# Second layer's experts: high and low parts as 128 stationary columns, and the product down spread over the next expert's steps

## The chip, the cores and the metric

The kernel runs on one core of one Trainium2 chip. The metric is the device time of one execution, in microseconds. Three runs of the kernel before took 2166.81, 2170.14 and 2172.33 us; the median, 2170.14 us, is the time that the change is held against. TensorE is PE (its weight loads PEld), VectorE is DVE, ScalarE is ACT, GpSimd is POOL and SyncE, which issues the loads of weights, is SP.

## The reference

Two layers, each with four mixers (Hyena, S5, RWKV, Mamba), a gated merge of their outputs and a mixture of 16 experts, on 256 latent and 256 context tokens of 1024 channels. The second layer has no context output. The change lies in the experts:

```
def moe_ffn(u, w_group, w_expert, w_gate, w_up, w_down):
    ...                          # groups by softmax, two experts of a group for each token
    comb = jnp.sum(jax.nn.one_hot(e_idx, MOE_EXPERTS, dtype=F32) * top_w[..., None], axis=-2)
    y = jnp.zeros_like(u)
    for e in range(MOE_EXPERTS):
        h = jax.nn.silu(u @ w_gate[e]) * (u @ w_up[e])
        y = y + comb[..., e:e + 1] * (h @ w_down[e])
    return y
```

For each expert w_gate and w_up are 1024 x 512 and w_down is 512 x 1024, all float32. In the second layer an expert's list has 64 places, so at most 64 tokens are computed in the main pass.

## The kernel before

A large float32 product is made of three products of shorter operands: each operand is split into a high part (a cast that rounds, on ACT, L299) and a low part (the operand less its high part, on DVE, L300), and `mm3` (L320) adds high by high, high by low and low by high in a bank of PSUM.

An expert has twelve chunks of weights of 512 KB each: four of gate, four of up, four of down (L1371 `expert`). Each chunk is loaded by SP into one of 21 buffers `raw`, taken in turn, cast by ACT into `wh` and subtracted by DVE into `wl`. There are three pairs of `wh` and `wl`, taken in turn, so ACT can cast a chunk only when PE has finished with the chunk three before it. PE then multiplies.

For gate and up the tokens are stationary and the weights move: the token columns `xx` of the expert (64 columns of the high or of the low part) are loaded as weights of the array, and 512 columns of `wh` or `wl` stream past them. A chunk holds two blocks of 128 channels, so it takes six matmuls of 512 columns. The result has 64 rows (tokens) and 512 columns. ACT takes the tanh of half the gate (L1403), DVE makes gate and up into h by two operations (L1404, L1405), PE transposes h in four pieces (L334) and ACT and DVE split the transposed 128 x 256 into `hh` and `hl`. For down `hh` and `hl` are stationary; a chunk takes six matmuls of 512 columns into two banks. ACT and DVE scale the two halves of the result into `yo` (L1417, L1418), and POOL scatters the rows to `Y` in memory (L1419).

The loop over experts (L1627 to L1646) sets the order: of each expert, three steps of gate (one chunk each), then the whole product down of the expert before it, then one further step of gate and four of up. With the fourth step `entries` (L1558) makes the list of the expert after next: which tokens, where they go (`ri`) and their weights (`rf`), each in a pool of four buffers. `ri` is read by the scatter of its expert. In the second layer `gather` (L1595) makes the token columns `xx` of four experts at a time by products with a matrix of picks; it runs beside experts 2 to 5, 6 to 9 and 10 to 13, in steps, and the last experts run without it.

The first layer's experts go through the same loop, with lists of 112 places and `xh`, `xl` in place of `xx`. A scheduler orders the instructions of each engine from the whole program by its own estimates; on the chip each engine takes them in that order and waits for what an instruction needs.

Of the kernel before, what the change touches and what calls it, by code (L numbers as in the profile page):

```python
# [24 lines left out]
# tiles of 128 columns of w_in: Hyena, S5, RWKV (r, k, v, wd | ad), Mamba (z, x, B, C), gates, then gd | dt  # L25
T_HY, T_S5, T_RW, T_WA, T_M2, T_GT, T_GDT, NTILE = 0, 6, 8, 14, 15, 23, 55, 56
EPS = 1e-6
AHEAD = 3
AH2 = 5
# [47 lines left out]
NQS = (2, 4)  # pairs of groups in a part of S5  # L77
# [3 lines left out]
# ---------------------------------------------------------------- constants of the shapes  # L81


def _cst():
# [16 lines left out]
    # N^T of two-token blocks, rows s, columns t; backward scans in partitions 0..63  # L101
# [15 lines left out]
    # places less 1024  # L117
# [3 lines left out]
    # a token's row in U, and in Y2 for its first and second expert; Y2's less that of the rows without a token  # L121
    c["tok"] = np.stack([tok + 1.0, tok, tok + 512.0, tok - 1024.0], 2).reshape(128, 16)
    # resets of the running sums at the ends of 64-token chunks
# [7 lines left out]
def _rows():  # L131
    """rows of the modulation in groups of 32 (context, latent; the bias in the first's third): to each token's stream, to latent"""
    half = np.r_[np.ones(64), np.zeros(64)]
    m = np.zeros((128, 2, 128))
    for p in range(0, 128, 32):
        m[p:p + 2, 0] = half, 1 - half
        m[p + 1, 1] = 1
    m[2] = 1
    return m.reshape(128, 256)
# [39 lines left out]
def pack(inp):  # L179
    """Lays the inputs out for the loads; no arithmetic on them."""  # L180
# [32 lines left out]
    # S5: rows (second index of a pair of groups, state), columns (part, direction, pair)  # L213
# [44 lines left out]
class K:  # L258
# [27 lines left out]
    def banks(self, **n):  # L286
        """the banks of PSUM by tag"""
# [9 lines left out]
    # ---- float32 operands of the large products in two parts of 12 bits: a b = ah bh + al bh + ah bl  # L297
# [4 lines left out]
    def raw(self, ap):  # L302
        """1024 columns of weights"""
# [7 lines left out]
    def wsplit(self, ap, k):  # L311
        """the parts of 1024 columns of weights (k by 1024 / k)"""
# [18 lines left out]
    def tr(self, out, in_, base=0):  # L331
        """out = in_^T on the tensor engine"""
# [6 lines left out]
    def rsqrt(self, pool, out, x, tag):  # L339
        """out = x ** -0.5 by Newton's iteration from the exponent's half; x > 0, small tiles"""  # L340
# [11 lines left out]
    def proj(self, l, t, xm, c0, c1, n=128):  # L352
        """p^T of w_in's tile t: n columns in partitions, tokens c0..c1"""
# [6 lines left out]
    # ------------------------------------------------------------------ RWKV-7  # L360
    def rwkv(self, l, xm, pc, dtT, yT, ctx_out, beside):
        """yT[:, hp, :]: the mixer's output, channels in partitions; columns 0..255 context, 256.. latent.
        dtT: Mamba's dt, from the tile that has both's columns, with tokens in partitions"""
        v, s, g, c = self.v, self.s, self.g, self.c
        with ExitStack() as es:
# [23 lines left out]
            def shifted(ps, n, j, out):  # L389
                """p + (mean of its neighbours - p) mu"""  # L390
# [20 lines left out]
            lo = {0: 64, 1: 0}  # partitions of the solves  # L411
# [4 lines left out]
            own = {d: slice(lo[d], lo[d] + 64) for d in range(2)}  # columns of a direction in the pairs' matrices  # L416
# [8 lines left out]
            for hp in range(2):  # L425
# [3 lines left out]
                # kappa: k k_k over its norm in the head  # L429
# [7 lines left out]
                # block diagonal pairs, of directions or heads: -b~ and k~ against kappa~, and the solves' (later M)  # L437
# [5 lines left out]
                for st in range(2):  # L443
# [6 lines left out]
                    for d in range(2):  # L450
                        dh = 2 * d + hp
                        # decay in log, its running sum in each chunk, and W = exp of that
# [21 lines left out]
                        s.activation(cum, cum, AF.Exp, scale=-1.0)  # 1 / W  # L474
# [16 lines left out]
                        # products of a chunk's tokens, masked: rows k~ and b~ (b~ and k~ backward)  # L491
# [11 lines left out]
                    # (I - N)^-1 of every chunk, N = -tril(kappa~ beta~^T): pairs of blocks, doubling  # L503
# [8 lines left out]
                    def each(a, b, us=range(8)):  # L512
                        """a^T b of the pairs"""
# [18 lines left out]
                    # tokens in partitions: v above (below) the solves, kappa~, and [k~; -b~]  # L532
# [33 lines left out]
                    # per chunk: H' = W_T (M H + k~^T v - b~^T u0), and y's reading of H  # L566
# [15 lines left out]
                    # the states that chunks enter (block diagonal), the last one that of the next stream's first chunk  # L582
# [23 lines left out]
                    # y^T  # L606
# [10 lines left out]
                    # group norm over a head, bonus, gate  # L617
# [24 lines left out]
    def headscale(self, pool, sq, f, eps, is_max, ni):  # L642
        """(f * sum over a head of sq, with eps added or as its least) ** -0.5, over the head's partitions"""
# [29 lines left out]
    def silu(self, x, t):  # L673
        """x = silu(x), with a scratch like it"""
# [4 lines left out]
    # ------------------------------------------------------------------ Mamba-2  # L679
    def mamba(self, es, l, xm, pc, yT, ctx_out, dtT):  # L680
# [4 lines left out]
        if True:  # L685
# [10 lines left out]
            # softplus = max(x, 0) + log1p(exp(-|x|)); log1p(e) = 2 atanh(e / (2 + e))  # L696
# [724 lines left out]
    def moe(self, l, m, x, pool, nt, rows, tabl, U, Y2, e_f, fp, tmp, ready, after):  # L1421
# [99 lines left out]
        with ExitStack() as es:  # L1521
# [33 lines left out]
            with ExitStack() as e2:  # L1555
# [72 lines left out]
                for e in range(16):  # L1628
# [6 lines left out]
                    for j in range(8):  # L1635
                        if j == AHEAD:
                            for _ in prev:
                                pass
# [324 lines left out]
```

## Time and profile before

| | |
|---|---|
| runs of the kernel before | 2166.81, 2170.14, 2172.33 us |
| span of the profiled execution, first to last instruction | 2165.3 us |
| lowest of the three runs less that span | 1.5 us |
| mean granted clock of TensorE, as a share of full | 0.946 |
| PE, DVE, ACT, POOL busy, share of the span | 91%, 76%, 46%, 18% |
| first scatter of the second layer's experts | at 1856.33 us |
| last one | at 2136.72 us |

The profiled execution has no time of its own beside its span; what lies around the span is read off the lowest run. Busy shares are means over all stages. In the second layer's experts the starts of the sixteen scatters mark the experts, one each. A matmul's duration includes its way through the array, so what a row of matmuls costs is the distance between their starts. The granted clock is given per window: 1.00 is 2.4 GHz, 0.50 is 1.2 GHz.

### The profile page before, as it was taken

What the parts mean: (1) busy time and instruction counts of PE and PEld (TensorE: products, weight loads), DVE (VectorE), ACT (ScalarE), POOL (GpSimd) and SP (SyncE); (2) the same over time, 40 slices, a digit from 0 to 9 for tenths busy, and PEclk for the clock granted to TensorE, in tenths of its full rate; (3) what the DMA queues carried; (4) which work ended last, traced back from release to release, by engine and by line L of the source; (5) the groups of instructions that cost most, each with busy time, mean ns of one, the idle gap of its engine ahead of it and who ended that gap; (6) DMA issues with size and microseconds to landing.
All of it is one profiled execution on the core that took longest, in us unless ns stands there. A gap on an engine that the chain in (4) does not pass through costs nothing. (4 is left out here: it accounts for less than half of the span.)

```text
span 2165.3 us, 31795 instructions
## 1 busy us (share of the span) xinstructions
PE 1970.2 (91%) x11290; PEld 1504.7 (69%) x11290; DVE 1651.0 (76%) x3451; ACT 985.5 (46%) x1571; POOL 399.0 (18%) x502
## 2 busy tenths in 40 slices
PE   6999999889999899999995899899798878999994
PEld 2779889567666678777774689897575767555652
DVE  5575675478888777999996686776879776888895
ACT  3321322244344234777773332323434335777783
POOL 1000100033532322102213010100524221010100
PEclk9999999889999898999998899999898988999997
DMA  7221221533444845999993221312434394899981
GB/s 299 78 74 59 74 67 52 197 123 113 156 146 154 313 172 186 362 368 372 372 341 138 84 90 63 98 52 76 160 134 161 129 350 174 304 329 366 330 325 64
DMA packets 131915, 406.28 MB, mean 188 GB/s; under 512 B 18139, under 2 KB 30205, under 8 KB 131361
## 3 DMA queue, kind: packets, MB, share of 16 engines
q1 hardware_dynamic: 125778, 388.34, 50.6%
q0 software_dynamic: 5968, 15.80, 2.3%
q8 instruction: 92, 1.51, 0.3%
q14 instruction: 77, 0.63, 0.1%
HBM read 374.72 MB, written 34.61 MB: 189 GB/s over the span
## 5 line engine op out<-in xcount | busy, mean ns | idle before, releaser
L299 ACT CAST wh<-raw 128x1024 fp32r<-128x1024 f32 x528 | 553.0, 1048 | 537.9 <-PE bank L337 482.9
L300 DVE TENSOR_TENSOR wl<-raw,wh 128x1024 fp32r<-128x1024 f32 x528 | 642.6, 1231 | 146.4 <-ACT wh L299 143.1
L337 PE MATMUL bank<-xmh,wh 128*128 128x512 f32 (+2 forms) x896 | 338.3, 378 | 15.8 <-ACT wh L299 14.7
L337 PE MATMUL bank<-xmh,wl 128*128 128x512 f32 (+2 forms) x896 | 331.0, 370 | 15.4 <-DVE wl L300 15.4
L337 PE MATMUL bank<-xml,wh 128*128 128x512 f32 (+2 forms) x896 | 326.4, 365 | 0.0
L337 PEld LDWEIGHTS bank<-xmh,wh 128*128 128x128 f32 (+1 forms) x896 | 176.7, 197 | 54.2 <-ACT wh L299 19.2
L337 PEld LDWEIGHTS bank<-xmh,wl 128*128 128x128 f32 (+1 forms) x896 | 175.9, 196 | 51.6 <-DVE wl L300 22.2
L337 PEld LDWEIGHTS bank<-xml,wh 128*128 128x128 f32 (+1 forms) x896 | 176.5, 197 | 29.2 <-issue 6.2
L337 PE MATMUL bank<-wh,xx 128*64 128x512 f32 x512 | 168.1, 397 | 0.2 <-ACT wh L299 0.2
L1419 POOL DMA_INDIRECT Y<-yo,ri x32 | 43.4, 1357 | 420.4 <-DVE yo L1418 304.8
L337 PE MATMUL bank<-DD,TB 128*128 128x64 f32 (+1 forms) x848 | 111.5, 273 | 1.3 <-DVE TB L523 0.9
L337 PEld LDWEIGHTS bank<-DD,TB 128*128 128x128 f32 x848 | 106.3, 192 | 6.0 <-DVE DD L598 0.9
L337 PE MATMUL bank<-wl,xx 128*64 128x512 f32 x256 | 102.8, 402 | 1.3 <-DVE wl L300 1.1
L337 PE MATMUL bank<-wl,hh 128*112 128x512 f32 (+1 forms) x256 | 99.9, 396 | 0.0
L337 PEld LDWEIGHTS bank<-wh,xx 128*64 128x64 f32 x512 | 69.6, 136 | 43.1 <-issue 1.4
L337 PE MATMUL bank<-wl,xh 128*112 128x512 f32 x240 | 97.9, 408 | 0.2
L337 PE MATMUL bank<-wh,hl 128*112 128x512 f32 (+1 forms) x256 | 97.4, 400 | 0.5 <-DVE hl L300 0.2
L337 PE MATMUL bank<-wh,xl 128*112 128x512 f32 x240 | 94.8, 395 | 0.9 <-DVE xl L300 0.9
L337 PE MATMUL bank<-wh,xh 128*112 128x512 f32 x240 | 92.8, 395 | 0.8 <-ACT xh L299 0.8
L337 PE MATMUL bank<-wh,hh 128*112 128x512 f32 (+1 forms) x256 | 89.8, 397 | 1.1 <-ACT hh L299 1.1
L337 PE MATMUL bank<-raw,c 128*32 128x256 f32 x768 | 71.3, 423 | 18.6 <-DMA raw<-in_modw_dram 18.6
L337 PE MATMUL bank<-DD,AB 128*128 128x64 f32 x640 | 84.5, 275 | 0.7 <-DVE DD L510 0.7
(547 smaller groups left out, 3799.5 us busy)
## 6 DMA issues: line engine op xcount, KB each, us to landing
raw<-in_mg_dram SPq DMA_DIRECT2D x128, 512.0 KB
raw<-in_mup_dram SPq DMA_DIRECT2D x128, 512.0 KB
raw<-in_mdn_dram SPq DMA_DIRECT2D x128, 512.0 KB
raw<-in_win_dram SPq DMA_DIRECT2D x112, 512.0 KB
raw<-in_modw_dram SPq DMA_DIRECT2D x96, 512.0 KB
GT<-t SPq DMA_DIRECT2D x32, 256.0 KB
raw<-in_wbr_dram SPq DMA_DIRECT2D x16, 512.0 KB
G<-GT SPq DMA_DIRECT2D x8, 1024.0 KB
```

The source lines that it names most:

```text
L299: self.s.copy(hi, src)
L300: (eng or self.v).tensor_tensor(lo, src, hi, OP.subtract)
L337: self.t.matmul(out, lhsT=lhsT, rhs=rhs, start=start, stop=stop)
L1419: g.indirect_dma_start(out=Y2, out_offset=bass.IndirectOffsetOnAxis(ap=to, axis=0), in_=yo, in_offset=None, bounds_check=1023, oob_is_err= ...
```

## The change

Five things change, and all comments and docstrings are gone, which moves line numbers by 2 to 32 lines (L299 is L301 now, L300 is L302, L337 is L339, L1403 to L1405 have L1425 to L1427 beside them).

1. `STEPS` gives the order of steps for each layer, g for a step of the present expert and p for one chunk of the product down of the one before. The first layer's string is the old order. In the second layer the four chunks of down stand apart: after the fourth, fifth, seventh and eighth step.
2. In the second layer `xx` holds an expert's high and low columns side by side, and `both` loads all 128 as stationary, so one matmul with `wh` makes high by high in rows 0 to 63 and low by high in rows 64 to 127. A second matmul of 64 columns adds high by low: two in place of three.
3. The two halves of the rows must be added, and h is needed transposed. ACT copies the 128 x 512 bank of gate and that of up into `gu` (L1420), and eight matmuls of 128 x 64 with two stacked identities (`i64`) add and transpose at once. The four transposes of h are gone; tanh and the two operations of DVE work on 128 x 256 in place of 64 x 512.
4. `ri` and `rf` have eight buffers in place of four.
5. `hh` and `hl` are taken from their pools ahead of the banks of gate and up.

```
+STEPS = ("gggppppggggg", "ggggpgpggpgp")
...
+        stacked = OC[l] and xs is not None
...
+        hh, hl = (tmp.tile([128, 4, cap], F32R, tag="h" + x, bufs=xb[2], name="h" + x) for x in "hl")
+        pg, pu = self.bank(), self.bank()
...
-                    self.mm3(ps, [z[:, kk] for z in xs], (wh[:, k], wl[:, k]), kk == 0, kk == KT - 1)
+                    if stacked:
+                        both = lambda: self.mm(ps, xs[:, kk], wh[:, k], kk == 0, kk == KT - 1)
+                        if kk < KT - 1:
+                            both()
+                        self.mm(ps[0:cap], xs[:, kk, 0:cap], wl[:, k], False, False)
+                        if kk == KT - 1:
+                            both()
+                    else:
+                        self.mm3(ps[0:cap], [z[:, kk] for z in xs], (wh[:, k], wl[:, k]), kk == 0, kk == KT - 1)
                 yield
...
+        if stacked:
+            pt = self.bank()
+            for j, ps in enumerate((pg, pu)):
+                r = tmp.tile([128, 512], F32, tag=f"gu{j}", bufs=1, name="gu")
+                s.copy(r, ps)
+                for k in range(4):
+                    self.mm(pt[:, 256 * j + 64 * k:256 * j + 64 * k + 64], r[:, 128 * k:128 * k + 128], self.c["i64"])
+            pg, pu = pt[:, 0:256], pt[:, 256:512]
+            h = tmp.tile([128, 256], F32, tag="h", bufs=xb[1], name="h")
+            s.activation(h, pg, AF.Tanh, scale=0.5)
+            v.scalar_tensor_tensor(h, h, 1.0, pg, OP.add, OP.mult)
+            v.scalar_tensor_tensor(h, h, 0.5, pu, OP.mult, OP.mult)
+            self.split(h.rearrange("p (k t) -> p k t", k=4), hh, hl)
...
                 self.mm3(py[b], (hh[:, kc], hl[:, kc]), [x[:, 0, 512 * b:512 * b + 512] for x in (wh, wl)], kc == 0, kc == 3)
+            if kc < 3:
+                yield
...
-                    ri = tmp.tile([128, 2], I32, tag="ri", bufs=4, name="ri")[0:cap]
-                    rf = tmp.tile([128, 1], F32, tag="rf", bufs=4, name="rf")[0:cap]
+                    ri = tmp.tile([128, 2], I32, tag="ri", bufs=8, name="ri")[0:cap]
+                    rf = tmp.tile([128, 1], F32, tag="rf", bufs=8, name="rf")[0:cap]
...
-                    for j in range(8):
-                        if j == AHEAD:
-                            for _ in prev:
-                                pass
-                            if e < 14:
-                                rec.append(turn("g", entries, e + 2, picks[e + 2]) if OC[l] else entries(e + 2))
+                    j = 0
+                    for z in STEPS[l]:
+                        if z == "p":
+                            next(prev, None)
+                            continue
+                        if j == AHEAD and e < 14:
+                            rec.append(turn("g", entries, e + 2, picks[e + 2]) if OC[l] else entries(e + 2))
```

On PE, in one of the last experts, the kernel before has the four transposes of the expert before, the end of the third step of gate, and then the product down in one block (xx: gate and up; hh and hl: down; 64x512 is the shape of the result):

```order
L334 MATMUL bank<-cst,h 128x64 x4
L337 MATMUL bank<-wl,xx 64x512
L337 MATMUL bank<-wh,xx 64x512 x2
L337 MATMUL bank<-wl,xx 64x512
L337 MATMUL bank<-wh,xx 64x512
L337 MATMUL bank<-wh,hh 64x512 x2
L337 MATMUL bank<-wl,hh 64x512 x2
L337 MATMUL bank<-wh,hl 64x512 x2
L337 MATMUL bank<-wh,hh 64x512
L337 MATMUL bank<-wl,hh 64x512
L337 MATMUL bank<-wh,hl 64x512
L337 MATMUL bank<-wh,hh 64x512
```

In the changed kernel the fourth step of gate ends and the first chunk of down follows; the first four matmuls of it are `hh` alone:

```order
L339 MATMUL bank<-wl,xx 64x512 x2
L339 MATMUL bank<-wh,xx 128x512
L339 MATMUL bank<-wh,hh 64x512
L339 MATMUL bank<-wl,hh 64x512
L339 MATMUL bank<-wh,hh 64x512
L339 MATMUL bank<-wl,hh 64x512
L339 MATMUL bank<-wh,xx 128x512
L339 MATMUL bank<-cst,gu 128x64 x4
L339 MATMUL bank<-wl,xx 64x512
L339 MATMUL bank<-wh,xx 128x512
L339 MATMUL bank<-wl,xx 64x512
L339 MATMUL bank<-wh,hl 64x512 x2
```

The product down no longer stands in one block: two chunks of up come between its matmuls, the products with `hl` come after the first of them, and the four that sum and transpose the `gu` of the gate stand inside that chunk.

On ACT, in the same place, one expert of the kernel before is, from the two casts ahead of the tanh on:

```order
L299 CAST wh<-raw 128x1024 x2
L1403 ACTIVATE h<-bank 64x512
L299 CAST wh<-raw 128x1024 x6
L299 CAST hh<-bank 128x256
L299 CAST wh<-raw 128x1024 x4
L1417 ACTIVATE yo<-bank,rf 64x512
L299 CAST wh<-raw 128x1024 x2
L1403 ACTIVATE h<-bank 64x512
```

In the changed kernel an expert has, from the scaling of `yo` to the next expert's:

```order
L1447 ACTIVATE yo<-bank,rf 64x512
L301 CAST wh<-raw 128x1024 x2
L1425 ACTIVATE h<-bank 128x256
L301 CAST wh<-raw 128x1024 x3
L1420 COPY gu<-bank 128x512
L301 CAST hh<-h 128x256
L301 CAST wh<-raw 128x1024 x7
L1420 COPY gu<-bank 128x512
L1447 ACTIVATE yo<-bank,rf 64x512
L301 CAST wh<-raw 128x1024 x2
```

Between the tanh of an expert and its `hh` there now stand three casts of weights and the copy `gu` of the next expert's gate (the tanh, the three casts, the copy and then `hh`, a cast of `h`); before, six casts stood between the tanh and `hh`, and no copy.

Elsewhere, with the sources of the other stages unchanged, the scheduler orders some instructions of the first layer's experts (the lists, the splits of tokens) and of the second layer's mixers and gates otherwise than before.

## Rows read from the trace of the kernel before

**Rows 1.** The page, part 1: busy us (share) x instructions of each engine.
```profile
PE 1970.2 (91%) x11290; PEld 1504.7 (69%) x11290; DVE 1651.0 (76%) x3451; ACT 985.5 (46%) x1571; POOL 399.0 (18%) x502
```

**Rows 2.** Timeline of POOL, second layer: start, us, engine, line, operation [idle before].
```profile
1856.33 1.18 POOL L1419 DMA_INDIRECT Y<-yo,ri  x1 [39.48 <-DVE yo L1418]
...
2051.83 2.30 POOL L1419 DMA_INDIRECT Y<-yo,ri  x1 [18.49 <-DVE yo L1418]
...
2120.89 1.16 POOL L1419 DMA_INDIRECT Y<-yo,ri  x1 [16.12 <-DVE yo L1418]
2136.72 0.90 POOL L1419 DMA_INDIRECT Y<-yo,ri  x1 [14.67 <-DVEq L1650]
```

**Rows 3.** Windows of 20 us: PE, PEld, DVE, ACT, POOL busy; PEclk, DMA share, GB/s.
```profile
1140.00:1160.00 20.00, 16.93 (x73) 11.77 (x71) 15.67 (x17) 13.54 (x16) 1.18 (x1) 1.00 0.15 46
1900.00:1920.00 20.00, 18.05 (x74) 9.90 (x73) 14.90 (x17) 12.54 (x15) 0.55 (x1) 0.91 0.85 295
2060.00:2080.00 20.00, 20.00 (x89) 11.23 (x88) 18.79 (x22) 15.54 (x19) 1.16 (x1) 1.00 1.01 389
```

**Rows 4.** Lines by form, 2034 to 2104.8 us: count | busy, mean ns | idle before.
```profile
L299 ACT CAST wh<-raw 128x1024 fp32r<-128x1024 f32 x49 | 51.3, 1048 | 14.4 <-PE bank L337 10.2 <-DMA raw<-in_mup_dram 1.9 <-DMA raw<-in_mdn_dram 1.5
L337 PE MATMUL bank<-wh,xx 128*64 128x512 f32 x130 | 41.9, 394 | 0.0
```

**Rows 5.** Timeline of DVE, one expert without a gather.
```profile
2071.19 3.48 DVE L300 TENSOR_TENSOR wl<-raw,wh 128x1024 fp32r<-128x1024 f32 x3
2074.60 0.67 DVE L1405 SCALAR_TENSOR_TENSOR h<-h,bank 64x512 f32<-64x512 f32 x1
2075.20 3.56 DVE L300 TENSOR_TENSOR wl<-raw,wh 128x1024 fp32r<-128x1024 f32 x3
```

**Rows 6.** Timeline of ACT, the same expert.
```profile
2077.40 0.37 ACT L299 CAST hh<-bank 128x256 fp32r<-128x256 f32 x1
...
2085.62 1.05 ACT L299 CAST wh<-raw 128x1024 fp32r<-128x1024 f32 x1 [0.22 <-PE bank L337]
2086.58 0.58 ACT L1403 ACTIVATE h<-bank 64x512 f32<-64x512 f32 x1
2087.07 1.04 ACT L299 CAST wh<-raw 128x1024 fp32r<-128x1024 f32 x1
```

**Rows 7.** Timeline of PE, merge of the branches: 128 stationary columns.
```profile
1797.83 0.40 PE L337 MATMUL bank<-wh,mh 128*128 128x512 f32 x1
1798.07 0.39 PE L337 MATMUL bank<-wl,mh 128*128 128x512 f32 x1
```

**Rows 8.** Timeline of PE, second layer's experts: 64 stationary columns.
```profile
2070.26 0.40 PE L337 MATMUL bank<-wl,xx 128*64 128x512 f32 x1
2070.49 0.62 PE L337 MATMUL bank<-wh,xx 128*64 128x512 f32 x2
```

**Rows 9.** Timeline of PE, a mixer: float32 products of 128x64.
```profile
205.15 1.06 PE L337 MATMUL bank<-DD,AB 128*128 128x64 f32 x8
```

**Rows 10.** Tile at: durations min/median/max of the copies out of a bank.
```profile
L1447 ACT COPY at<-bank x16: 573/586/593, 801.6 to 1810.5; 128x512 f32<-128x512 f32 x16
```

**Rows 11.** Waits of the second layer's experts, 1856 to 2137 us: in all, times, longest.
```profile
ACT wh L299 <- PE bank L337: 49.7, 97, 2.9
...
DVE ri L1575 <- DMA Y<-yo,ri: 8.2, 4, 3.1
```

**Rows 12.** Timeline of PE, a wait after which the clock held.
```profile
1882.19 0.39 PE L337 MATMUL bank<-rent,pick 128*64 128x3 f32 x4 [1.07 <-DVE rf L1582]
1883.33 0.45 PE L337 MATMUL bank<-wl,xx 128*64 128x512 f32 x1 [0.36 <-DVE wl L300]
```

**Rows 13.** Timeline of PE, a wait after which the clock fell.
```profile
1904.08 0.51 PE L337 MATMUL bank<-pick,uh 128*128 128x256 f32 x2 [1.56 <-DVE rf L1582]
...
1906.09 0.63 PE L337 MATMUL bank<-wl,xx 128*64 128x512 f32 x1
...
1909.08 0.69 PE L337 MATMUL bank<-wh,xx 128*64 128x512 f32 x2
```

More of the change, by code (lines that the diff above doesn't have):

```diff
@@ L1393, in expert @@
             xs = xh, xl
-        pg, pu = self.bank()[0:cap], self.bank()[0:cap]
+        hh, hl = (tmp.tile([128, 4, cap], F32R, tag="h" + x, bufs=xb[2], name="h" + x) for x in "hl")
+        pg, pu = self.bank(), self.bank()
         for nm, ps in (("mg", pg), ("mup", pu)):
@@ L1399, in expert @@
                     kk = 2 * kc + k
-                    self.mm3(ps, [z[:, kk] for z in xs], (wh[:, k], wl[:, k]), kk == 0, kk == KT - 1)
-                yield
-        h = tmp.tile([128, 512], F32, tag="h", bufs=xb[1], name="h")[0:cap]
-        s.activation(h, pg, AF.Tanh, scale=0.5)
-        v.scalar_tensor_tensor(h, h, 1.0, pg, OP.add, OP.mult)
-        v.scalar_tensor_tensor(h, h, 0.5, pu, OP.mult, OP.mult)
-        ps = self.bank()
-        for k in range(4):
-            self.tr(ps[:, cap * k:cap * k + cap], h[:, 128 * k:128 * k + 128])
@@ L1409, in expert @@
-        hh, hl = (tmp.tile([128, 4, cap], F32R, tag="h" + x, bufs=xb[2], name="h" + x) for x in "hl")
-        self.split(ps[:, 0:4 * cap].rearrange("p (k t) -> p k t", k=4), hh, hl)
+                    if stacked:
[7 more added lines that the diff above has]
+                        self.mm3(ps[0:cap], [z[:, kk] for z in xs], (wh[:, k], wl[:, k]), kk == 0, kk == KT - 1)
@@ new lines, in expert @@
+                yield
+        if stacked:
[11 more added lines that the diff above has]
+            self.split(h.rearrange("p (k t) -> p k t", k=4), hh, hl)
+        else:
+            pg, pu = pg[0:cap], pu[0:cap]
+            h = tmp.tile([128, 512], F32, tag="h", bufs=xb[1], name="h")[0:cap]
+            s.activation(h, pg, AF.Tanh, scale=0.5)
+            v.scalar_tensor_tensor(h, h, 1.0, pg, OP.add, OP.mult)
+            v.scalar_tensor_tensor(h, h, 0.5, pu, OP.mult, OP.mult)
+            ps = self.bank()
+            for k in range(4):
+                self.tr(ps[:, cap * k:cap * k + cap], h[:, 128 * k:128 * k + 128])
+            self.split(ps[:, 0:4 * cap].rearrange("p (k t) -> p k t", k=4), hh, hl)
@@ L1599, in gather @@
                                     slot[:, :, 4 * q:4 * q + 4].unsqueeze(3).to_broadcast([128, T, 4, 64]), OP.is_equal)
-                    xx = [tmp.tile([128, KT, 2, 128], F32R, tag="xx", bufs=3, name="xx") for _ in range(2)]
+                    xx = [tmp.tile([128, KT, 2, 2, 64], F32R, tag="xx", bufs=3, name="xx") for _ in range(2)]
                     for j in range(4):
                         picks.append([pick[:, i, j].bitcast(F32) for i in range(T)])
-                        xs.append([xx[j // 2][:, :, z, 64 * (j % 2):64 * (j % 2) + 64] for z in range(2)])
+                        xs.append(xx[j // 2][:, :, j % 2].rearrange("p k z t -> p k (z t)"))
                     for k in range(KT):
@@ L1609, in gather @@
                         for j in range(2):
-                            s.copy(xx[j][:, k], ps.rearrange("p (z j t) -> p j z t", z=2, j=2)[:, j])
+                            s.copy(xx[j][:, k], ps.rearrange("p (z j i t) -> p j i z t", z=2, j=2, i=2)[:, j])
                         yield
@@ L1626, in moe @@
                     rec = [entries(0, [pick0[:, i] for i in range(T)]), r1]
-                prev = ()
+                prev = iter(())
                 for e in range(16):
@@ L1643, in moe @@
                             next(side, None)
+                        j += 1
                     prev = this
```

## Prediction

> **What bounds the kernel now.** I read the page's first part, then the scatters of POOL, which cut the second layer's experts into sixteen pieces, then windows and groups of lines of that stage, then the timelines of single experts. PE is busy for 91% of the span [rows 1]. The first scatter starts at 1856.33 us, the eleventh at 2051.83, the fifteenth at 2120.89, the last at 2136.72 [rows 2]. So the ten intervals that carry a gather or its rest take 195.5 us, 19.55 each, the four without take 69.06, 17.27 each, and the last takes 15.83. In a window of experts without a gather PE is busy all 20 us, DVE 18.79, ACT 15.54, the DMA share is 1.01 at 389 GB/s, the clock 1.00 [rows 3]. PE is the bound there, and DVE and the loads stand close behind it: that is the first thing to see, since a change that takes work from PE can win only up to them.
>
> PE's 17.27 us are accounted for: an expert has 12 chunks of six matmuls, 72 of 512 columns, each of which lasts 0.39 us with its way through the array and none of which PE came to late [rows 4], and which start 0.23 us apart (2070.26 to 2070.49) [rows 8]; with 0.2315, between the 0.229 and 0.233 that longer runs of such starts give, that is 16.67, and transposes and lists make the rest, 0.6.
>
> **The change part by part.**
>
> *Two matmuls for three.* 128 stationary columns cost no more than 64: in the merge of the branches the starts are 0.24 us apart (1797.83 to 1798.07) [rows 7], against 0.23 [rows 8]. Gate and up fall from 48 matmuls to 32 for an expert. The eight summing products of 128x64 are float32 products as in the mixers, where eight take 1.06 us with the last one's way through the array [rows 9]; less that (0.27) the step is 0.113, so they cost 0.9. The four transposes go (about 0.3), the lists stay (0.3). PE's work is then 56 x 0.2315 + 0.9 + 0.3 = 14.2 us, 3.1 less. If every idle stretch could be filled this would be worth 16 x 3.1 = 49 us; the other engines forbid that.
>
> *The other engines.* DVE: a subtraction occupies 1.137 us ((2074.60 - 2071.19) / 3) and an operation on 64x512 0.60 [rows 5]. Twelve subtractions are 13.64; the operations on 128x256 I take at half of 0.60 each, as the free size halves; hl, yo and the lists, with one long operation and three short ones, I put at two operations of that size, 1.2: 15.4 in place of 16.0. ACT: a cast occupies 0.96 and tanh 0.49 [rows 6]; the copies gu have their like in a copy of a 128x512 bank, 0.59 [rows 10]. Twelve casts (11.5), two copies (1.2 at most), half a tanh (0.25), hh (0.3) and yo (like the tanh, 0.5) make about 13.7, and before, without the copies and with the whole tanh, 12.8. Loads: 6.29 MB an expert at the 389 GB/s of [rows 3] are 16.2 us. None of these reaches 17.27, so by work alone the next bound is 16.2.
>
> *The order.* Here I leave the work and follow the queues of the changed kernel. ACT may cast a chunk only when PE is done with the chunk three before it; that already makes ACT wait 49.7 us in this stage [rows 11]. The first chunk of down stands on PE directly behind the fourth of gate, and its first matmul needs hh. On ACT there stand, behind the tanh: three casts, the copy gu of the gate, hh. The third of those casts (the second chunk of down) takes the buffers of the fourth chunk of gate, so it starts only when PE ends that chunk. From there PE waits for a cast (0.95), the copy (0.59) and hh (0.37 [rows 6]): 1.9 us in which it has nothing to do, since it takes its queue in order. Of an opposite kind is the next one: ACT's cast of the third chunk of up needs the buffers of the first chunk of down, and the products with hl, which release them, stand behind the first chunk of up; ACT idles some 2 us, and PE, when it comes to the next chunk of down, waits 0.25 and 0.72 for casts; twice 0.25 more goes on subtractions that come late in gate. In sum 1.9 + 0.25 + 0.72 + 0.5 = 3.4 us of idle per expert. 14.2 + 3.4 = 17.6, with the handovers partly beside the work 17.5. That stands against 17.27: the matmuls saved come back as idle. Bounds: none of the idle (then 16.2, by the loads) and all of it with the ACT queue late once more by a cast (18.5). I take 17.5, since casts, copy and hh in a row are fixed by the order and their durations are measured.
>
> *Lists with eight buffers.* DVE waits 8.2 us in four waits for a scatter to release ri [rows 11], all beside gathers; eight buffers end that, 0.82 for each of the ten intervals. What else a gather adds (19.55 - 17.27 - 0.82 = 1.46: its products, casts, picks) stays.
>
> *Ends.* The first scatter comes after sixteen chunks of gate and up and four of down instead of eleven and four: 64 + 24 = 88 matmuls for 90, but with 3.4 idle and the sums: +4 us, while little is known of this start (bounds 0 and +6). The last expert is short: at its predecessor's scatter its gate and up are nearly done already; what is left is a copy, sums, tanh, two operations of DVE, hh (together 3.2), 24 matmuls of down (5.6) and yo (0.7 and a handover), 10.0 in place of 15.83: -5.8.
>
> *Clock.* When PE waits, its clock can fall. At 1904 us PE had been idle 1.56 us for a list; from 1906.09 to 1909.08 seven matmuls then took 2.99 us, 0.43 each in place of 0.23 [rows 13], and the window has a granted clock of 0.91 [rows 3]. At 1882 it had been idle 1.07 and then 0.36 and the clock held [rows 12]. That is half the rate (1.2 GHz); the seven lost 1.4 us, with the partly slow ones at both ends some 1.7. The changed kernel idles 1.9 us once per expert, and is nearer the first case. But at 1140 us a window of PE busy 16.93 of 20 has a clock of 1.00 [rows 3], with idle time scattered. Ends: no fall, and sixteen falls (27 us). I take five, 8.5 us: between the ends, nearer the low one because most of the idle is cut by short pieces of work.
>
> The Trainium skill ("TensorE: Matmul & The Clock Gate", section "HAM oscillation — how this bites in real kernels") describes a loop whose TensorE idles for a transfer in every round, is throttled to the cold clock each time and pays half of the throttled time. The trace agrees for one of two waits of this sort. [...]
>
> *Other stages.* The first layer's experts keep their step order and their matmuls, and the scheduler's other order of lists and mixers moves work that is not on one chain; I cost it at nothing, with ±6 us for the range, as nothing in the trace gives its sign.
>
> *Sum.* Ten intervals at 17.5 + 1.46 = 18.96 for 19.55: -5.9. Four at 17.5 for 17.27: +0.9. Last: -5.8. First: +4. Clock: +8.5. In all +1.7. The profiled span is 2165.3 us, 1.5 below the lowest run and 4.8 below the median; the sum is a difference, and against the median it gives 2170.1 + 1.7 = **2172 us**. About 0.3%, 6.5 us, is what a measurement here can tell from no change, so I forecast no change that can be told.
>
> **Rivals.**
>
> *The idle does not come.* For it: before, ACT waited for PE, not PE for ACT, and any hh or cast that is ready earlier than I place it lets PE run on. Against it: the third cast before hh cannot start before PE is done with the last chunk of gate. Then the loads bound, 16.2: ten intervals at 17.66 (-18.9), four at 16.2 (-4.3), the last -5.8, the first +0.6: -28, **2142**. With half of the idle left some 2155.
>
> *The clock falls in every expert (slower).* One mechanism: the 1.9 us before hh, the sixteen low stretches behind it, 1.7 us each. In place of +8.5 it is +27: -6.8 + 27 = +20, **2190**. The other terms are -6.8, so the result is slower by 6.5 us from the eighth fall on. For it [rows 13], against it [rows 12] and the window at 1140 us.
>
> *The change does little in this stage, and the new order elsewhere decides*: the idle is hidden to the same extent as before and the sum near zero, with ±6 us and more from the first layer's experts: 2160 to 2182.
>
> **How the numbers follow.** Forecast, idle with up to seven falls, 0.50 (2160 to 2185, of it faster 0.08, same 0.27, slower 0.15). No idle or half of it 0.24, all faster. A fall in nearly every expert 0.19, all slower (to 2200). The order elsewhere 0.07 (0.03, 0.02, 0.02). In sum faster 0.35, same 0.29, slower 0.36. The range 2147 to 2196 leaves out the fastest part of the first rival (about 0.12) and the end of the second (0.07); the likeliest case alone spans 2160 to 2185.
>
> **What would show it.** Right: in the timeline of PE a wait of about 1.9 us, released by ACT's hh, behind each fourth chunk of gate; scatters 17.5 us apart in the last experts; ACT idle about 2 us before a cast of up; no wait of ri for Y; DVE under 90% in these windows; windows with a clock of 0.9 or so. Wrong: windows with PE idle but scatters 16.2 apart and the DMA share at 1.0 throughout (then the first rival); clock under 0.9 in most windows and scatters over 19 apart (the second); a first scatter that moves by more than 6 us against the stage's start (then the stages before decide).

## The result, and the profile after

The changed kernel takes 2187.37 us, the median of four runs (2186.24 to 2188.21), against 2170.36 us of the kernel before: a ratio of 1.0082, 95% interval 1.0067 to 1.0098. It is slower by 17 us, clear of what can be told from no change. The time lies in the forecast's range, but in the part of it that belonged to the slow rival; the forecast itself was 2172 us. The spans of the two profiled executions differ by 20.8 us (2186.1 and 2165.3), and the account below is of these.

The page's first part, against [rows 1]: PE is busy 18.6 us less, and the kernel is slower all the same.

```profile
PE 1951.6 (89%) x11226; PEld 1512.3 (69%) x11226; DVE 1644.4 (75%) x3451; ACT 992.4 (45%) x1603; POOL 395.4 (18%) x502
```

The scatters of POOL, against [rows 2] (start, duration, and in brackets the idle time before):

```profile
1859.86 0.99 POOL L1449 DMA_INDIRECT Y<-yo,ri  x1 [46.69 <-DVE rf L1612]
...
2067.21 1.36 POOL L1449 DMA_INDIRECT Y<-yo,ri  x1 [17.48 <-ACT wh L301]
2087.67 1.37 POOL L1449 DMA_INDIRECT Y<-yo,ri  x1 [19.10 <-ACT wh L301]
2107.25 1.50 POOL L1449 DMA_INDIRECT Y<-yo,ri  x1 [18.21 <-ACT wh L301]
2125.41 1.37 POOL L1449 DMA_INDIRECT Y<-yo,ri  x1 [16.66 <-ACT wh L301]
2145.01 1.16 POOL L1449 DMA_INDIRECT Y<-yo,ri  x1 [18.23 <-ACT yo L1447]
2156.74 0.90 POOL L1449 DMA_INDIRECT Y<-yo,ri  x1 [10.57 <-DVEq L1682]
```

From the first to the eleventh it is 207.35 us where it was 195.5, from there to the fifteenth 77.80 where it was 69.06, and the last takes 11.73 where it took 15.83. The first starts 3.5 us later. The intervals without a gather are no longer alike: 18.16 at best (2107.25 to 2125.41), 20.46 and 19.58 in others.

The windows (PE, PEld, DVE, ACT, POOL busy; granted clock, DMA share, GB/s), against [rows 3]:

```profile
2060.00:2080.00 20.00, 16.93 (x72) 10.49 (x71) 15.44 (x17) 14.19 (x17) 1.36 (x1) 0.91 0.90 325
2080.00:2100.00 20.00, 16.89 (x67) 9.75 (x67) 16.20 (x17) 14.19 (x17) 1.37 (x1) 0.91 0.94 333
2100.00:2120.00 20.00, 17.43 (x82) 10.89 (x81) 16.38 (x18) 15.95 (x19) 1.50 (x1) 1.00 0.81 296
```

In none of them is an engine busy throughout, and the DMA share has fallen below 1. A chain has taken the place of the bound. A granted clock of 0.91 for 20 us is one fall to half the rate (1.2 GHz) for 3.4 us; there are ten such falls in the stage, two of them in its first and last experts, where the kernel before had two in all.

The chain is seen where ACT and PE are laid beside each other. First ACT, from the tanh of an expert on:

```profile
2107.57 0.38 ACT L1425 ACTIVATE h<-bank 128x256 f32<-128x256 f32 x1
2107.84 1.99 ACT L301 CAST wh<-raw 128x1024 fp32r<-128x1024 f32 x2
2110.12 1.04 ACT L301 CAST wh<-raw 128x1024 fp32r<-128x1024 f32 x1 [0.29 <-PE bank L339]
2111.07 0.58 ACT L1420 COPY gu<-bank 128x512 f32<-128x512 f32 x1
2111.55 0.41 ACT L301 CAST hh<-h 128x256 fp32r<-128x256 f32 x1
2113.88 3.13 ACT L301 CAST wh<-raw 128x1024 fp32r<-128x1024 f32 x3 [1.92 <-PE bank L339]
```

Then PE (the sums of `gu`; the last matmul of the fourth chunk of gate; the first of down; the first chunk of up; the first products with `hl`; the first of down's third chunk, in brackets the idle time before and what ended it):

```profile
2106.28 1.00 PE L339 MATMUL bank<-cst,gu 128*128 128x64 f32 x8
...
2109.68 0.40 PE L339 MATMUL bank<-wh,xx 128*128 128x512 f32 x1
2112.01 0.44 PE L339 MATMUL bank<-wh,hh 128*64 128x512 f32 x1 [1.93 <-ACT hh L301]
...
2113.21 0.40 PE L339 MATMUL bank<-wl,xx 128*64 128x512 f32 x1
2113.45 0.39 PE L339 MATMUL bank<-wh,xx 128*128 128x512 f32 x1
2113.68 0.39 PE L339 MATMUL bank<-wl,xx 128*64 128x512 f32 x1
2113.90 0.62 PE L339 MATMUL bank<-wh,hl 128*64 128x512 f32 x2
...
2117.06 0.68 PE L339 MATMUL bank<-wh,hh 128*64 128x512 f32 x2 [0.64 <-ACT wh L301]
```

PE ends the fourth chunk of gate at 2110.08. The third cast behind the tanh starts at 2110.12, since it needs that chunk's buffers; the copy follows at 2111.07, `hh` at 2111.55, and PE goes on at 2112.01. ACT then idles 1.92 us, until the chunk of up behind this has released its `wh`: the last product with it ends at 2113.84, the cast starts at 2113.88. The waits of the whole stage (in all, times, longest):

```profile
ACT wh L301 <- PE bank L339: 73.1, 58, 4.4
...
PE bank L339 <- ACT hh L301: 24.8, 12, 3.6
```

Before, ACT waited for PE in 97 short pieces, 49.7 us in all [rows 11]; now it is 58 longer ones, 73.1 us, and PE waits for ACT as well. The wait of `ri` for a scatter is gone.

### The profile page after: what moved, and what is told of

It reads as the page before. It is cut to its first block, busy times and chain, and to the rows that moved or that the text cites. A ratio compares the mean times of both kernels' runs of the same rounds, so it can differ in the third digit from the quotient of the medians.

```text
span 2186.1 us, 31721 instructions
## 1 busy us (share of the span) xinstructions
PE 1951.6 (89%) x11226; PEld 1512.3 (69%) x11226; DVE 1644.4 (75%) x3451; ACT 992.4 (45%) x1603; POOL 395.4 (18%) x502
## 5 line engine op out<-in xcount | busy, mean ns | idle before, releaser
L301 ACT CAST wh<-raw 128x1024 fp32r<-128x1024 f32 x528 | 548.7, 1049 | 544.6 <-PE bank L339 487.7
L302 DVE TENSOR_TENSOR wl<-raw,wh 128x1024 fp32r<-128x1024 f32 x528 | 642.1, 1235 | 183.3 <-ACT wh L301 180.4
L339 PE MATMUL bank<-xmh,wh 128*128 128x512 f32 (+2 forms) x896 | 335.2, 375 | 12.4 <-ACT wh L301 11.1
L339 PE MATMUL bank<-xmh,wl 128*128 128x512 f32 (+2 forms) x896 | 330.0, 369 | 13.3 <-DVE wl L302 13.3
L339 PE MATMUL bank<-xml,wh 128*128 128x512 f32 (+2 forms) x896 | 324.2, 362 | 0.0
L339 PEld LDWEIGHTS bank<-xmh,wl 128*128 128x128 f32 (+1 forms) x896 | 174.9, 195 | 49.8 <-DVE wl L302 20.3
L339 PEld LDWEIGHTS bank<-xmh,wh 128*128 128x128 f32 (+1 forms) x896 | 175.1, 196 | 49.3 <-ACT wh L301 15.3
L339 PEld LDWEIGHTS bank<-xml,wh 128*128 128x128 f32 (+1 forms) x896 | 174.9, 195 | 27.6 <-issue 4.7
L339 PE MATMUL bank<-wh,hh 128*112 128x512 f32 (+1 forms) x256 | 94.9, 408 | 37.5 <-ACT hh L301 27.8
L339 PE MATMUL bank<-DD,TB 128*128 128x64 f32 (+1 forms) x848 | 111.5, 273 | 1.3 <-DVE TB L525 0.9
L339 PEld LDWEIGHTS bank<-DD,TB 128*128 128x128 f32 x848 | 106.2, 191 | 6.1 <-DVE DD L600 0.9
L339 PE MATMUL bank<-wl,xx 128*64 128x512 f32 x256 | 102.0, 418 | 3.8 <-DVE wl L302 3.7
L339 PE MATMUL bank<-wh,xx 128*128 128x512 f32 x256 | 103.6, 413 | 0.1
L339 PE MATMUL bank<-wl,hh 128*112 128x512 f32 (+1 forms) x256 | 103.5, 405 | 0.1
L339 PE MATMUL bank<-wh,hl 128*112 128x512 f32 (+1 forms) x256 | 98.9, 407 | 0.4 <-DVE hl L302 0.4
L339 PE MATMUL bank<-wl,xh 128*112 128x512 f32 x240 | 98.0, 408 | 0.0
L339 PE MATMUL bank<-wh,xl 128*112 128x512 f32 x240 | 94.6, 394 | 0.0
L339 PE MATMUL bank<-wh,xh 128*112 128x512 f32 x240 | 92.4, 394 | 0.0
L339 PE MATMUL bank<-raw,c 128*32 128x256 f32 x768 | 69.3, 426 | 20.2 <-DMA raw<-in_modw_dram 19.7
L339 PE MATMUL bank<-DD,AB 128*128 128x64 f32 x640 | 84.4, 275 | 0.7 <-DVE DD L512 0.7
L339 PEld LDWEIGHTS bank<-wh,hh 128*112 128x112 f32 (+1 forms) x256 | 38.5, 157 | 65.0 <-ACT hh L301 33.9
```

Of the source, the lines that this page charges most:

```text
L301: self.s.copy(hi, src)
L302: (eng or self.v).tensor_tensor(lo, src, hi, OP.subtract)
L339: self.t.matmul(out, lhsT=lhsT, rhs=rhs, start=start, stop=stop)
```

## The experiments

Each is compared with the kernel before, run beside it on the same chip; the ratio has its 95% interval. The theory is that of the chain: PE waits for `hh` behind casts and a copy on ACT, and its clock falls in such waits. Rival A: the spreading of down costs, by itself. Rival B: the work of copies and sums costs, wherever it stands.

**Stacking without the spreading** (`e1_block`)

```
-STEPS = ("gggppppggggg", "ggggpgpggpgp")
+STEPS = ("gggppppggggg", "gggppppggggg")
```

> The changed kernel with the old order of steps in the second layer (three steps of gate, then all four chunks of down), the stacking and the lists kept. Theory (PE waits for hh: stacking makes the way from the last chunk of up to hh longer by two copies and eight sums, and PE has only the chunks in between to fill it): with three chunks of four matmuls ahead of down instead of four, PE waits longer for hh, 3 us or more per expert instead of 1.93, scatters 19.5 us or more apart without a gather, clock falls in most experts, 2187 to 2205 us. Rival A (the stacking is good by itself and the spreading of down is what costs, since a chunk of down that waits holds the buffers of the chunks of up): without the spreading the idle goes and PE's lesser work shows, scatters 16 to 17 us apart, 2140 to 2160 us.

2206.38 us, 1.0154 (1.0131 to 1.0177): slower still, and 1 us past the theory's upper bound. In this order the chain is longer; the timeline of ACT around one `hh`:

```profile
2101.26 0.38 ACT L1425 ACTIVATE h<-bank 128x256 f32<-128x256 f32 x1
2101.54 1.04 ACT L301 CAST wh<-raw 128x1024 fp32r<-128x1024 f32 x1
2104.64 0.40 ACT L301 CAST hh<-h 128x256 fp32r<-128x256 f32 x1 [2.06 <-DVE h L1427]
```

The first matmul of down in PE's timeline, at the same place:

```profile
2105.10 0.69 PE L339 MATMUL bank<-wh,hh 128*64 128x512 f32 x1 [3.77 <-ACT hh L301]
```

The waits of PE for `hh` over the stage (in all, times, longest):

```profile
PE bank L339 <- ACT hh L301: 41.4, 11, 4.3
```

Here ACT itself waits 2.06 us for DVE's h: the way from up over copies, sums, tanh and DVE to `hh` takes longer than PE needs for three chunks of gate at two matmuls for three. Rival A falls: with the stacking, the spreading is what softens the loss.

**Spreading without the stacking** (`e2_spread`)

```
-        stacked = OC[l] and xs is not None
+        stacked = False
```

(with `mm3` taking the two halves of `xx` as before; the lists keep their eight buffers)

> The changed kernel without the stacking (three matmuls with 64 stationary columns, four transposes, no copies and no sums), with the spread order and the lists of eight buffers. Theory: hh is ready when PE comes to it, PE is busy throughout and bound at 17.2 us per expert, no wait for hh over 0.5 us, no falls but at the end; the lists win some 8 to 10 us and the short last expert 7, the later first scatter loses 5 to 7: 2156 to 2166 us. Rival A (spreading costs): waits for casts as in the changed kernel, scatters over 18 us apart, 2175 to 2190 us.

2158.60 us, 0.9942 (0.9922 to 0.9963), as the theory has it. The scatters around the last gather and behind it:

```profile
2013.06 2.43 POOL L1449 DMA_INDIRECT Y<-yo,ri  x1 [15.30 <-ACT wh L301]
2034.71 3.76 POOL L1449 DMA_INDIRECT Y<-yo,ri  x1 [19.23 <-ACT wh L301]
2052.32 2.30 POOL L1449 DMA_INDIRECT Y<-yo,ri  x1 [13.84 <-ACT hh L301]
2069.92 2.29 POOL L1449 DMA_INDIRECT Y<-yo,ri  x1 [15.30 <-ACT hh L301]
```

17.6 us without a gather, and 21.66 in the interval in which a gather starts: in the spread order the steps of a gather fall into one interval. The eight buffers of the lists alone give as much (2156.95 us, the next run), so no gain of the spreading by itself is shown.

**The lists alone** (`e3_lists`): the kernel before with

```
-                    ri = tmp.tile([128, 2], I32, tag="ri", bufs=4, name="ri")[0:cap]
-                    rf = tmp.tile([128, 1], F32, tag="rf", bufs=4, name="rf")[0:cap]
+                    ri = tmp.tile([128, 2], I32, tag="ri", bufs=8, name="ri")[0:cap]
+                    rf = tmp.tile([128, 1], F32, tag="rf", bufs=8, name="rf")[0:cap]
```

> The kernel before with eight buffers for ri and rf in place of four, nothing else. Theory: the four waits of DVE for a scatter (8.2 us) and the one fall of the clock behind them (1.4 us) go: 2159 to 2164 us. Rival (they are given back later, as the loads or PE then wait elsewhere): 2168 to 2172 us.

2156.95 us, 0.9934 (0.9913 to 0.9955), a little more than the theory had. It wins 13 us, and the lists alone are the best of the change's parts: 30 us under the whole. Without a gather nothing changes:

```profile
2045.92 1.16 POOL L1419 DMA_INDIRECT Y<-yo,ri  x1 [17.56 <-DVE yo L1418]
2063.19 1.16 POOL L1419 DMA_INDIRECT Y<-yo,ri  x1 [16.11 <-DVE yo L1418]
```

**`hh` cast by DVE** (`e5_hhdve`): the changed kernel with

```
-            self.split(h.rearrange("p (k t) -> p k t", k=4), hh, hl)
+            h4 = h.rearrange("p (k t) -> p k t", k=4)
+            v.tensor_copy(hh, h4)
+            v.tensor_tensor(hl, h4, hh, OP.subtract)
```

> The changed kernel, but hh of the second layer is cast by DVE directly behind its second operation on h, so that it stands behind no cast of weights and no copy on ACT. Theory: hh is ready about 0.5 to 1 us sooner, the wait of PE for hh falls from 1.93 to 1.0 to 1.4 us, fewer falls of the clock (under five instead of ten in the stage), 2165 to 2178 us. Rival B (the added work of the copies and sums, 1.8 us of PE and 1.2 us of ACT per expert, sets the time, not the place of hh): no change, 2183 to 2190 us.

2190.73 us, 1.0087 (1.0067 to 1.0107): no change, as Rival B had it, and the theory's number was missed. The trace says why the experiment doesn't decide. The timeline of DVE (h, a subtraction, `hh`):

```profile
2115.49 0.42 DVE L1427 SCALAR_TENSOR_TENSOR h<-h,bank 128x256 f32<-128x256 f32 x1
2115.82 1.22 DVE L302 TENSOR_TENSOR wl<-raw,wh 128x1024 fp32r<-128x1024 f32 x1
2116.95 0.29 DVE L1429 CAST hh<-h 128x256 fp32r<-128x256 f32 x1
```

The first matmul of down on PE, in the same expert:

```profile
2117.39 0.46 PE L339 MATMUL bank<-wh,hh 128*64 128x512 f32 x1 [2.32 <-DVE hh L1429]
```

The scheduler put a subtraction of 1.13 us between h and `hh`, so `hh` came no sooner than on ACT, and PE waited 2.32 us. The wait was moved to another queue, not taken away.

**Down later** (`e5_late`, `e6_down_last`): the changed kernel with copies, sums and stacking as they are, and

```
-STEPS = ("gggppppggggg", "ggggpgpggpgp")
+STEPS = ("gggppppggggg", "ggggpggggppp")
```

or `"gggggggpgppp"` as the second string.

> The changed kernel with another order of steps in the second layer: one chunk of down after the fourth step of gate, the other three after the eighth step (ggggpggggppp). Copies, sums, stacking and lists are those of the changed kernel. In the order of the queues hh now stands behind three casts and no copy, and no cast ahead of it waits for the last chunk of gate. Theory (the wait for hh and the clock falls behind it cost the time, not the added work): waits of PE for hh under 0.7 us, at most three falls in the stage, scatters 16 to 17 us apart without a gather, 2143 to 2158 us, under both kernels. Rival B (the work of copies and sums sets the time): scatters stay at 18 us or more, 2178 us or more.

> The changed kernel with down later still: one chunk after the seventh step, three after the eighth (gggggggpgppp). Theory: hh has three more chunks of time than in the changed kernel, no wait for it, scatters 16 to 17 us apart, 2143 to 2160 us. Rival B: 2178 us or more. If both orders without the wait are alike, it is the wait and not a certain order that counts.

2141.04 us, 0.9871 (0.9850 to 0.9892), and 2141.88 us, 0.9863 (0.9841 to 0.9885): both under both kernels, 1 to 2 us under the theory's ranges, and 42 to 46 us under the changed kernel (2183.75 us when it was run again below, 2187.37 at first) with the same work. Rival B falls. The scatters of the first of them, without a gather:

```profile
2016.36 6.37 POOL L1449 DMA_INDIRECT Y<-yo,ri  x1 [17.47 <-DVE h L1427]
2032.31 1.65 POOL L1449 DMA_INDIRECT Y<-yo,ri  x1 [9.58 <-ACT wh L301]
2048.42 1.66 POOL L1449 DMA_INDIRECT Y<-yo,ri  x1 [14.46 <-ACT wh L301]
```

Its windows, columns as above:

```profile
1900.00:1920.00 20.00, 18.91 (x93) 12.81 (x94) 19.50 (x21) 17.58 (x22) 3.66 (x2) 1.00 1.02 403
2020.00:2040.00 20.00, 18.77 (x93) 12.39 (x92) 19.58 (x20) 17.55 (x22) 4.38 (x2) 1.00 1.02 407
2040.00:2060.00 20.00, 18.95 (x83) 11.16 (x82) 19.54 (x20) 17.77 (x22) 1.66 (x1) 1.00 1.01 399
```

Its waits over the stage:

```profile
ACT wh L301 <- PE bank L339: 19.3, 40, 1.0
...
PE bank L339 <- ACT hh L301: 1.8, 1, 1.8
```

PE waits for `hh` once, at the end; there is no fall between the first scatter and the last; scatters without a gather come 16 to 17 us apart up to the thirteenth (the last three, 26.28, 8.49 and 5.01 us, come unevenly); DVE is busy 19.5 of 20 us and the DMA share is 1.01 or 1.02 at 399 to 407 GB/s. That is the bound of the loads that the first rival named (2142 us), reached by another order, with DVE nearly as full.

**Four pairs of wh and wl** (`e7_four`): the changed kernel with

```
-MPT = ("xmg", "xmg")
+MPT = ("xmg", "xmgy")
-NZ = (4, 5)
+NZ = (4, 3)
```

(and two letters `z` fewer in the second string of `MST`, to match), which leaves 19 buffers of `raw` in place of 21.

> The changed kernel with four pairs of wh and wl in turn and three fewer... two fewer buffers of raw weights (19 in the ring). The order of steps is that of the changed kernel. Theory: the third cast ahead of hh needs the buffers of the third chunk of gate, not of the fourth, so hh comes about 1 us sooner in most experts; the wait for hh falls under 1.5 us in half of them and with it the falls: 2160 to 2178 us. Rival B (work sets the time): 2183 us or more; rival C (the loads need the buffers): waits of ACT for loads, 2187 us or more.

2160.14 us, 0.9952 (0.9936 to 0.9969), at the lower edge of the theory's range: a cast now waits for the chunk four before it and not three. The scheduler's order changed with it, and the waits for `hh` are fewer, not shorter (1865 to 2105 us: in all, times, longest):

```profile
PE bank L339 <- ACT hh L301: 16.5, 7, 3.5
```

Seven in place of nine in the same stretch of the changed kernel. That four pairs with the order that came with them win 24 to 27 us is shown; how much of it is the buffers' and how much the new order's is not.

**Sums in one pass** (`e8_onepass`): `gu` and the identities as operands of the short kind.

```
-                r = tmp.tile([128, 512], F32, tag=f"gu{j}", bufs=1, name="gu")
+                r = tmp.tile([128, 512], F32R, tag=f"gu{j}", bufs=1, name="gu")
...
-                    self.mm(pt[:, 256 * j + 64 * k:256 * j + 64 * k + 64], r[:, 128 * k:128 * k + 128], self.c["i64"])
+                    self.mm(pt[:, 256 * j + 64 * k:256 * j + 64 * k + 64], r[:, 128 * k:128 * k + 128], self.i64r)
```

(`i64r` is a rounded copy of the identities.)

> The changed kernel with gu and the identities rounded to the short operands of the other products, so that a sum takes one pass of PE in place of two; this leaves out the low part of the sums' operands. Order and waits stay. Theory: PE has 0.9 us less work per expert, but half of it lies beside waits that stay (hh is late as before), so 5 to 9 us come off: 2178 to 2183 us, with the wait for hh still at 1.5 to 2 us. Rival B: all of the 0.9 us shows, 14 us, 2172 us or less.

2179.77 us, 1.0055 (1.0034 to 1.0075): the theory's number, but its interval meets that of the changed kernel repeated below (1.0038 to 1.0080), so a gain of some us is likely and not shown. Of the 10.8 us between the spans of the two profiles (2175.3 and 2186.1) 6.4 lie ahead of the first product of the second layer's gate (at 1815.78 and 1822.18 us), where the sums have no part. The timeline of PE shows a sum's four matmuls as four records, where they were eight above, and the wait as it was:

```profile
2096.10 0.53 PE L339 MATMUL bank<-i64r,gu 128*128 128x64 f32 x4
...
2102.15 0.44 PE L339 MATMUL bank<-wh,hh 128*64 128x512 f32 x1 [1.93 <-ACT hh L301]
```

**The clock** (`e9_busy`, `e10_busy2`, and the changed kernel again, `e11_same`): three or two more matmuls per expert in the wait for `hh` (the edit shown is the one with two).

```
         py = [self.bank()[0:cap], self.bank()[0:cap]]
+        if stacked:
+            for _ in range(2):
+                self.mm(py[0][:, 0:256], self.c["i64"], h)
```

> The changed kernel with three more float32 matmuls of 64x256 per expert on PE, between the fourth chunk of gate and the first of down, from h into a bank that the product down then starts over; they use nothing that a later instruction waits for, and stand in the wait for hh. The order of the other instructions is that of the changed kernel. Theory (a part of the loss is the clock that falls after the wait of 1.93 us, some 1.45 us each): PE idles only some 0.9 us before h is there, the falls drop from ten to three or fewer, the wait for hh itself stays (PE comes to hh at the same time), intervals that had a fall are 1 to 1.5 us shorter, in all 8 to 12 us: 2174 to 2181 us. Rival D (falls lie beside waits and cost nothing in the end, or follow the shorter waits too): no change or slower by the added work, 2185 to 2195 us.

> As the run with three added matmuls on h per expert, with two. In that run the three took 1.5 us, about 0.5 us longer than the rest of the wait for hh, which ate some 8 us of what nine fewer falls gave. Two take 1.0 us, as long as hh takes behind h. Theory (the falls cost 1.4 us each): no falls but at the ends, intervals of 18.2 to 18.6 us without a gather, 8 to 13 us under the changed kernel in the same call. Rival D (falls cost nothing in the end): within 4 us of the changed kernel.

> The changed kernel itself, on the same chip as the run with two added matmuls, for a comparison within one call: 2183 to 2190 us by every theory.

Three: 2185.04 us, 1.0077 (1.0053 to 1.0101). Two: 2179.51 us, 1.0039 (1.0022 to 1.0056), with the changed kernel, run beside it on the same chip, at 2183.75 us, 1.0059 (1.0038 to 1.0080). By these times the theory was missed both times: it had 2174 to 2181 us for three, where Rival D had 2185 to 2195, and 8 to 13 us under the changed kernel for two, where 4.2 were measured and Rival D had up to 4. The traces say more. The added matmuls in PE's timeline, three of them (six records):

```profile
2085.16 1.48 PE L339 MATMUL bank<-h,cst 128*64 128x256 f32 x6 [0.98 <-DVE h L1427]
```

Two of them (four records):

```profile
2104.63 1.08 PE L339 MATMUL bank<-h,cst 128*64 128x256 f32 x4 [0.89 <-DVE h L1427]
```

A window of the run with two, at a place where the changed kernel has a fall:

```profile
2060.00:2080.00 20.00, 18.10 (x82) 10.69 (x81) 16.70 (x18) 14.92 (x18) 1.37 (x1) 1.00 0.91 337
```

The added ones wait for h, so PE idles 0.98 or 0.89 us and then works; after that there is no fall between the first scatter and the start of the last expert, where the changed kernel has eight. Three take 1.48 us, until 0.5 us after `hh` is there; two take 1.08 and end with it. With two the stretch from the first scatter to the last is 285.1 us, in the changed kernel run beside it 296.9: 11.8 us, with eight falls fewer between these scatters and one that stays. The way to the first scatter is 2.3 us longer with the added matmuls, and the spans differ by 9.1 us (2178.2 and 2187.3). By the medians it is 4.2 us. The two ratio intervals overlap, but nine of the ten executions with two added matmuls (at most 2181.78 us) lie under all six of the changed kernel (at least 2181.95), so a gain is shown.

In the changed kernel a fall followed eight of the eleven waits of 1.92 us, and in the two runs with added matmuls none of the twenty waits of 0.88 to 1.00 us. So the wait matters but does not decide alone: three waits of 1.92 us passed without a fall, and why those three is open. A fall costs 1.4 to 1.6 us in its interval: in the repeated run the second interval of a gather's four is 21.60 with a fall and 20.16 without, and with two added matmuls, without a fall, 20.03 and 20.18. How much of it reaches the time of the whole is between 4 and 12 us.

## Why the prediction was right or wrong

The forecast, no change that can be told, was missed: the kernel is 17 us slower (among the chances slower had 0.36, the same 0.29). The range held. That the time comes near the slow rival's 2190 is luck: that rival had sixteen falls at 1.7 us each, 27 us, and the ten falls in the stage, eight more than before, explain about half of the loss; the rest is experts that take longer without a fall too. By its steps:

- *The order: right to a tenth.* Three casts, a copy and `hh` ahead of the first matmul of down, the third cast tied to the end of the fourth chunk of gate: 1.9 us were worked out, 1.92 or 1.93 measured in eleven experts. ACT's idle of 2 us ahead of the next cast was 1.92, but the cast waited for the chunk of up (done at 2113.84) and not for the products with `hl`, which start at 2113.90. PE's wait at a later chunk of down was 0.63 to 0.91 for the 0.72 of the sum.
- *Two matmuls for three: right*, behind a matmul with 128 columns (2113.45) the next starts 0.23 us later, behind one with 64 (2113.21) 0.24. *The sums: wrong by half.* The step "eight take 1.06 us" read eight records as eight products; one float32 product is two records, so a sum of four takes 0.8 us (2106.28 to 2107.09) and an expert's eight cost 1.6 to 1.7 us, not 0.9. The run with one pass shows that little of it reached the end.
- *17.5 us without a gather: too small.* Of the four such intervals one has no fall; it takes 18.16 us. The run with two added matmuls, which has no fall in any of the four, has 18.92, 18.04, 18.18 and 17.87. In the interval of 18.16 PE is busy 15.60 us, where the sum had 14.2, and idle 2.57 us (1.93 and 0.64), where it had 3.4. The run with one pass has 18.06 in the same place: busy 14.89 and idle 3.16, so work that is taken from PE comes back as idle. The chain through ACT and DVE sets this step, and adding PE's work and waits was the wrong form of sum.
- *18.96 us with a gather: the step that failed by the most.* Measured 20.7. The sum took the gather's work as spread evenly. In the spread order it falls into one interval of four (21.5, 21.8 and 22.2 us), without a fall in any of the three. There PE is busy for 93% (19.86, 20.31 and 20.66 us) and no wait of 1.92 us is left, while in the other three of the four the chain sets the pace (17.23 busy of 20.17): what one lacks the others can't give. The scatters of the spreading alone show the same shape, with PE busy throughout the long intervals (21.65 of 21.65 us in the last).
- *Lists: right in kind.* The wait of `ri` is gone. The sum gave it 8.2 us; alone it brings 13.
- *Ends: near by the number, the first of them by luck.* The last expert took 11.73 us for 10.0. The first scatter came 3.5 us later, +4 in the sum. But the stage itself began 3.7 us sooner than before, which the sum, with the other stages at nothing, did not have. The first product of the gate, before and after:

```profile
1825.85 0.63 PE L337 MATMUL bank<-wh,xx 128*64 128x512 f32 x1
1822.18 0.63 PE L339 MATMUL bank<-wh,xx 128*128 128x512 f32 x1
```

So the way from there to the first scatter grew by 7.2 us (37.7 for 30.5), over the bound of +6: the first `hh` keeps PE waiting for 2.46 us, and a fall stands there too:

```profile
1844.42 0.69 PE L339 MATMUL bank<-wh,hh 128*64 128x512 f32 x1 [2.46 <-ACT hh L301]
```

- *Clock: the count was too low, the price of one fall too high.* Five falls more were taken, at 1.7 us each, and it is eight more, at some 1.4. The weight given to the fact that idle time was cut by short pieces of work was wrong; the wait after which the clock had fallen before [rows 13] was the right pattern, and the one after which it held [rows 12] was shorter, like the 0.9 us that the added matmuls leave. In time the term came out near, 9.8 us between the scatters for 8.5.

Together, with 1.4 us for a fall: between the scatters there are seven falls more than before, 9.8 us for the 8.5 taken (+1.3). Ten intervals came to +11.85 for -5.9, less four falls (+12.1). Four came to +8.74 for +0.9, less three falls (+3.6). The last, the first (with a fall of its own, and the sooner start) and the stretch behind the last scatter (+0.8) make +2.0. With the +1.7 forecast the sum is 20.7 of the 20.8 us between the spans.

The first rival, 2142 us if the idle did not come, was the price of the change with another order of steps, and two such orders met it (2141.04 and 2141.88). From the first product of the gate to the last scatter the stage takes 334.6 us where it took 310.9, 23.7 more; the stages ahead gave 3.7 back.

Open: which instructions of the chain set the 18.16 us; why three of the eleven waits passed without a fall; what part of the four pairs' gain is the buffers'; and whether a fall's cost reaches the median in full.

## What to carry to other kernels

Work taken from the bound engine pays only as far as the chain that replaces it allows: write down what stands ahead of the first instruction that needs the new result, on each queue, and which buffer the last of these waits for. When a chain is lengthened, give it more work of others to hide behind (here three of the four chunks of down behind the eighth step, over 40 us) before judging the change. Try the small part of a change alone; here it was worth more than the whole.

## What the runs showed of the hardware

In the changed kernel an idle stretch of 1.92 us on PE was followed by a fall of the clock to 1.2 GHz for 3.4 us in eight of eleven experts; where added matmuls cut the idle stretch down to 0.88 to 1.00 us there was none in twenty. A fall lengthened the interval in which it stood by 1.4 to 1.6 us.

A float32 product of 128x64 is recorded as two matmuls that start 0.11 us apart; one with short operands as one (2106.28 and 2096.10 us above, eight records and four for four products).
